# First stage of a two-layer backbone: order of the modulation loads, a last tile in two banks, rotary sines on another engine, a tie at the norm

## The chip, the cores and the metric

The kernel runs on one core of one Trainium2 chip. Its metric is device time in microseconds (us), the median of repeated executions. The engines are TensorE (PE in the profile), VectorE (DVE), ScalarE (ACT), GpSimd (POOL) and SyncE (SP), which here only issues loads and stores.

## The reference

A trunk of two layers on 1024 tokens of width 1024, with 256 context tokens. Layer 0 is windowed grouped-query attention with rotary positions and the context as a prefix; layer 1 is a Conformer convolution module. Each layer is an RMSNorm, shifted, scaled and gated by a linear map of the condition c (the "modulation"); a last RMSNorm ends it. Cut to what the change touches:

```python
shift, scale, gate = jnp.split((silu_c @ ada_w[i] + ada_b[i])[:, None, :], 3, axis=-1)
h_lat = modulate(rmsnorm(x, norm_g[i]), shift, scale)      # h * (1 + scale) + shift
proj = h_lat @ w_in                                         # layer 0
q = apply_rope(split_heads(proj[..., :q_end], N_Q_HEADS), cos, sin)
k = apply_rope(split_heads(proj[..., q_end:k_end], N_KV_HEADS), cos, sin)
v = split_heads(proj[..., k_end:v_end], N_KV_HEADS)
...
u = jax.nn.silu(layernorm(u, ln_g, ln_b))                   # layer 1
return (u * jax.nn.silu(z)) @ w_out
x = x + gate * y
```

## The kernel before, in words

**Numbers and tiles.** An fp32 product is made of three matmuls of split operands: high by high, low by high, high by low (`hh`, `hl` for activations, `whi`, `wlo` for weights). ScalarE writes a high part by a copy to the short form, VectorE or GpSimd the low part by a subtraction (`split_lo`, line 159). The width of 1024 is cut into eight tiles of 128 (`kt` 0 to 7), the tokens into two halves of 512.

**Program order.** Every instruction goes through one small wrapper, `InOrder`, so all of them carry its line, L89, in the profile; they are told apart by the names of their tiles. Where the wrapper is on, an engine's instructions keep the order in which the code is written: TensorE, VectorE and ScalarE through the whole first stage (`pin("PVA")`), TensorE alone after it (`pin("P")`), where a scheduler sets the order of the others. Each engine then works through its own queue strictly from the front.

**The loads of the first stage** (lines 318 to 345) stand in one queue on SP, 512 KB each: x rows 0 to 511 (four), `ada_load(0)` (the modulation's weights of tile 0, two transfers into `araw` pages), the first weight of the input projection (`wsA.load()`, a `wraw` page), `ada_load(1)`, the second and the third weight, `ada_load(2)` to `(5)`, x rows 512 to 1023, `ada_load(6)`, `(7)`, the context rows, and smaller things. Eight transfers are under way at a time: a further one is issued when the one eight places ahead has landed.

**The first half of the tokens** (lines 500 to 615). For each tile kt: `ada_row` multiplies the condition by the tile's modulation weights (16 small matmuls, `pso<-araw,c`, and a VectorE copy to an `arow` row); `turn` puts the x rows across by four transposes into one bank (`psg`); `ada_cols` turns the modulation row to columns (two pairs of tiny matmuls, `pso<-ident,arow`, and two VectorE rows that write `mod`); `x_tile` makes the modulated tile: ScalarE the high part `hh`, then VectorE the full value `hf` from the same bank, then VectorE `hl = hf - hh`; and `x_mm` adds its three products into the accumulators of the three weight chunks: 0 (k), 1 (q of the first group) and 2 (v). In between, `scale_rows` scales the x rows by their norm on ScalarE, `wsA.split` splits a weight (`whi` on ScalarE, `wlo` on VectorE, and from the fifth weight on `wlo` on GpSimd), and ScalarE squares the other rows for their norm.

**The second half** (lines 1172 to 1210) takes its x already turned (`xt`): VectorE `hf` (`x_f`), ScalarE `hh` (`x_h`), VectorE `hl` (`x_l`). Between its tiles stand two further streams. The context tiles (`c_tile`): two transposes, ScalarE `hf` and `hch`, VectorE `hcl`. And `rope` for the first half's k and q (lines 899 to 933): ScalarE copies the accumulator, SP swaps its halves by transfers (`rope_half`), VectorE multiplies by the cosine, GpSimd by the sine, and later, popped one at a time from the queue `ropes0` in tiles 4 to 7, VectorE adds the two, ScalarE writes the high part (`kh`, `qh`) and VectorE the low one (`kl`, `ql`). Then the first scores follow.

**The attention** (from line 1240) goes through heads and blocks: scores, softmax on the other engines, transposes, products with the values, and `fill(n)`, which puts n matmuls of the next projections (`psg`) into the gaps. At every fourth head (three times, at 267, 456 and 645 us) a *regroup* makes the next group's keys and values: `job("k")`, `job("v")`, `pv`, then `scores(*nxt)` and `vlate.pop(g)()`, which turns the last values by four transposes (`pso<-ident,vf_half`) and splits them (`vh`, `vl`).

**The norm of layer 1** (`layer_norm`, line 1467, for each half of the tokens): the squares are summed by VectorE, and across the partitions by PE (`pso<-ones,qa_half`); then VectorE `ms`, ScalarE the root `sq`, VectorE `rr` (reciprocal), `rq`, `rq`, `r`, and PE spreads r by `pso<-ident,r`. Around it runs the output projection, whose operands are split by `g_split` (line 1650; `gs` pages, high on ScalarE, low on VectorE) and `w_split` (`woh`, ScalarE).

## Time and profile before

| | |
|---|---|
| median of 3 runs | 1690.53 us (1690.23 to 1690.90) |
| the profiled execution, its own time | 1691.56 us |
| its span in the trace | 1689.8 us |
| granted TensorE clock | 0.999 |
| busy: PE, VectorE, ScalarE, GpSimd | 99%, 66%, 52%, 52% |
| transfers in the first fortieth of the span (42 us) | 385 GB/s, mean of the whole 145 |

A line of the trace reads: start in us from the start of the span, duration in us, engine, line, operation, what is written <- what is read, shape, how often, and in brackets how long the engine stood idle just before and what ended that idle time. SPq is SP's queue of issues. A line of waits reads: engine and tile, what was waited for, us in total, times, longest. A line of the chain of waits reads: start, duration, what was under way.

### The profile page before, as it was taken

The page shows a single profiled execution, that of the slowest core. Times are in us where ns is not written, and L with a number is a line of the kernel's source. Part 1 is how long each engine was busy: PE and PEld are TensorE (multiplying, and loading weights), DVE is VectorE, ACT ScalarE, POOL GpSimd, SP SyncE. Part 2 cuts the span into 40 slices and gives each one's busy share as a digit, 9 for nine tenths or more (in the row PEclk, how much of TensorE's full clock was granted, in tenths as well). Part 3 has the DMA queues.
Part 4 walks back from the last instruction along what each step waited for, and adds up shares of the span by engine and source line. Part 5 has one row for each costly group of instructions (what it writes and reads, how often), then busy time and mean ns, then how long its engine had stood idle before and what let it go on. Part 6 is the DMA issues. An engine that isn't in the chain of part 4 may idle for free.

```text
span 1689.8 us, 23975 instructions
## 1 busy us (share of the span) xinstructions
PE 1676.0 (99%) x8436; PEld 1413.9 (84%) x8436; DVE 1120.5 (66%) x2126; ACT 881.6 (52%) x1556; POOL 874.3 (52%) x724
## 2 busy tenths in 40 slices
PE   9999999999999999999999999999999999999998
PEld 6788888888888888888888888888888888888886
DVE  4756554656355654566324299999999999858832
ACT  5655543555355543556334365555665654566741
POOL 0166653666366663652101268999898887130400
PEclk9999999999999999999999999999999999999999
DMA  9424442544345443447976622020211212477881
GB/s 385 147 83 142 144 127 83 164 144 135 96 133 161 143 137 97 138 122 249 319 240 225 219 90 92 13 74 15 75 50 51 81 34 79 131 263 245 316 296 50
DMA packets 114776, 244.55 MB, mean 145 GB/s; under 512 B 11626, under 2 KB 36514, under 8 KB 114656
## 3 DMA queue, kind: packets, MB, share of 16 engines
q1 hardware_dynamic: 108576, 233.06, 41.0%
q10 hardware_dynamic: 6080, 9.97, 2.4%
q8 instruction: 66, 1.08, 0.3%
q14 instruction: 54, 0.44, 0.1%
HBM read 190.80 MB, written 41.69 MB: 138 GB/s over the span
## 4 chain that ended last, share of the span: by engine, by line
PE 92%; DMA 4%; DVE 2%; ACT 1%; issue 1%; SPq 0%; DVEq 0%; ACTq 0%
PE psg L89 50%; PE pss L89 21%; PE pso L89 21%; DMA wo_page<-in_conv_w_out_dram 1%; DMA araw_page<-in_k_ada_dram 1%; DMA x_page<-in_ctx_dram 1%; DMA x_page<-in_x_dram 1%; DVE pso L89 1%; DVE v_page L89 1%; DMA zsd<-sig_page 0%; DVE hf_page L89 0%; DMA wsum_raw<-in_ada_w_dram 0%; SPq L89 0%; ACT hh_page L89 0%; ACT gs_page L89 0%
## 5 line engine op out<-in xcount | busy, mean ns | idle before, releaser
L89 POOL TENSOR_TENSOR odd_half<-odd_half,prod_half 128x513 f32<-128x513 f32 (+2 forms) x252 | 315.0, 1258 | 22.0 <-ACT prod_half L89 8.5
L89 PE MATMUL psg<-hh_page,whi_page 128*128 128x512 f32 x600 | 235.5, 392 | 0.0
L89 PE MATMUL psg<-hl_page,whi_page 128*128 128x512 f32 x600 | 234.4, 391 | 0.0
L89 PE MATMUL psg<-hh_page,wlo_page 128*128 128x512 f32 x600 | 234.0, 390 | 0.0
L89 POOL TENSOR_TENSOR wlo_page<-wraw_page,whi_page 128x512 fp32r<-128x512 f32 (+1 forms) x104 | 172.1, 1670 | 113.7 <-ACT whi_page L89 52.9
L89 ACT ACTIVATE prod_half<-ubuf,dww 128x513 f32<-128x513 f32 (+2 forms) x252 | 165.7, 675 | 115.9 <-POOL odd_half L89 111.9
L89 PE MATMUL psg<-h2h_page,whi_page 128*128 128x512 f32 x464 | 181.9, 392 | 0.0
L89 PE MATMUL psg<-h2h_page,wlo_page 128*128 128x512 f32 x464 | 180.6, 389 | 0.0
L89 PE MATMUL psg<-h2l_page,whi_page 128*128 128x512 f32 x464 | 180.6, 389 | 0.0
L89 POOL TENSOR_SCALAR p_page<-p_page,sc 128x640 f32<-128x640 f32 (+1 forms) x128 | 100.2, 783 | 147.2 <-DVE sc L89 133.2
L89 DVE SCALAR_TENSOR_TENSOR pss<-ubuf,dww,pss 128x512 f32<-128x512 f32 (+3 forms) x270 | 172.4, 671 | 0.1
L89 DVE SCALAR_TENSOR_TENSOR pss<-ubuf,wsum,pss 128x512 f32<-128x512 f32 (+3 forms) x270 | 171.7, 671 | 0.2
L89 ACT ACTIVATE p_page<-p_page,sc 128x641 f32<-128x641 f32 (+1 forms) x128 | 102.9, 804 | 95.2 <-DVE sc L89 92.3
L89 ACT ACTIVATE pthi<-pss 128x512 fp32r<-128x512 f32 (+2 forms) x144 | 87.4, 619 | 111.0 <-PE pss L89 104.5
L89 DVE TENSOR_TENSOR ptlo<-pss,pthi 128x512 fp32r<-128x512 f32 (+2 forms) x144 | 101.8, 716 | 63.4 <-ACT pthi L89 62.2
L89 PEld LDWEIGHTS psg<-hh_page,wlo_page 128*128 128x128 f32 x600 | 112.6, 188 | 24.5
L89 PEld LDWEIGHTS psg<-hh_page,whi_page 128*128 128x128 f32 x600 | 112.8, 188 | 19.4
L89 PEld LDWEIGHTS psg<-hl_page,whi_page 128*128 128x128 f32 x600 | 112.8, 188 | 18.4
L89 POOL TENSOR_TENSOR rope_half<-rope_half,sin_page 128x512 f32<-128x512 f32 x40 | 52.1, 1302 | 142.1 <-DMA rope_half<-rope_half 68.8
L89 ACT ACTIVATE whi_page<-wraw_page 128x1024 fp32r<-128x1024 f32 x88 | 92.6, 1052 | 49.4 <-PE psg L89 21.6
L89 PE MATMUL pso<-h2h_page,whi_page 128*128 128x512 f32 x304 | 118.3, 389 | 0.0
L89 PE MATMUL pso<-h2l_page,whi_page 128*128 128x512 f32 x304 | 118.3, 389 | 0.0
(258 smaller groups left out, 4070.2 us busy)
## 6 DMA issues: line engine op xcount, KB each, us to landing
wraw_page<-in_k_wconv_dram SPq DMA_DIRECT2D x48, 512.0 KB, 3.2
wraw_page<-in_k_win_dram SPq DMA_DIRECT2D x40, 512.0 KB, 3.8
wo_page<-in_attn_w_out_dram SPq DMA_DIRECT2D x32, 512.0 KB, 6.2
wol_page<-wolA SPq DMA_DIRECT2D x32, 512.0 KB, 8.6
wo_page<-in_conv_w_out_dram SPq DMA_DIRECT2D x32, 512.0 KB, 7.3
wol_page<-wolC SPq DMA_DIRECT2D x32, 512.0 KB, 6.7
rope_half<-rope_half ACTq DMA_DIRECT2D x76, 128.0 KB, 2.4
araw_page<-in_k_ada_dram SPq DMA_DIRECT2D x16, 512.0 KB, 10.0
```

Source lines behind the costliest of these rows:

```text
L89: r = f(*a, **k)
```

## The change

It has seven parts. (1) `ada_load(2)` stands ahead of the third weight's load, and `ada_load(6)` between two pairs of x rows. (2) In the first half, the scaling of the last two x rows, tile 2's `ada_row` and its `ada_cols` stand ahead of the third weight's split, and tile 1's `ada_cols` stands one matmul earlier. (3) Tile 7's four transposes go into two banks, two each; ScalarE makes the high part of one half of the tokens while VectorE makes the full value of the other, then they swap, and one subtraction follows. (4) For the first half's k and q, the product with the sine is made by VectorE, in the popped pieces, which now are (product and sum) and (high and low part), and they are popped behind the context tiles. (5) The gate's first weight (z) is loaded and split one tile earlier. (6) At a regroup, the last values are turned and split only behind the next but one scores and three fills. (7) The low parts of `g_split` are tied to stand behind the layer norm's `ms`.

The places that matter, as the engines' queues have them. SP's queue in the first stage (araw: the modulation, two transfers per tile; wraw: the weights; x: token rows), before:

```order
L89 DMA wraw_page_109<-in_k_win_dram 128x1024
L89 DMA wraw_page_111<-in_k_win_dram 128x1024
L89 DMA araw_page_114<-in_k_ada_dram 128x1024
L89 DMA araw_page_115<-in_k_ada_dram 128x1024
L89 DMA araw_page_118<-in_k_ada_dram 128x1024
L89 DMA araw_page_119<-in_k_ada_dram 128x1024
```

and now:

```order
L89 DMA wraw_page_109<-in_k_win_dram 128x1024
L89 DMA araw_page_112<-in_k_ada_dram 128x1024
L89 DMA araw_page_113<-in_k_ada_dram 128x1024
L89 DMA wraw_page_116<-in_k_win_dram 128x1024
L89 DMA araw_page_118<-in_k_ada_dram 128x1024
L89 DMA araw_page_119<-in_k_ada_dram 128x1024
```

Tile 2's two transfers moved up by one place and the third weight down by two; tile 3's (118, 119) stay. VectorE's queue at tile 2, before:

```order
L89 COPY arow_half_113<-pso_321 128x256
L89 TENSOR_TENSOR wlo_page_317<-wraw_page_111,whi_page_316 128x1024
L89 TENSOR_SCALAR mod_177<-pso_338,bcol 128x2
L89 TENSOR_SCALAR mod_177<-pso_338,bcol,vt 128x2
L89 TENSOR_SCALAR hf_page_345<-psg_306,mod_177 128x512
L89 TENSOR_TENSOR hl_page_344<-hf_page_345,hh_page_343 128x512
```

and now:

```order
L89 COPY arow_half_111<-pso_318 128x256
L89 TENSOR_SCALAR mod_177<-pso_330,bcol 128x2
L89 TENSOR_SCALAR mod_177<-pso_330,bcol,vt 128x2
L89 TENSOR_TENSOR wlo_page_336<-wraw_page_116,whi_page_335 128x1024
L89 TENSOR_SCALAR hf_page_345<-psg_306,mod_177 128x512
L89 TENSOR_TENSOR hl_page_344<-hf_page_345,hh_page_343 128x512
```

The two `mod` rows moved ahead of the third weight's low part. VectorE's queue at the second norm (ms, rr, rq, r are the norm's; gs the output projection's splits), before:

```order
L89 TENSOR_TENSOR gs_page_14764<-v_page_13480,gs_page_14764 128x512
L89 TENSOR_SCALAR ms_789_14482<-pso_14477 128x4
L89 TENSOR_TENSOR gs_page_14659<-v_page_12324,gs_page_14659 128x512
L89 RECIPROCAL rr_791_14486<-sq_790_14484 128x4
L89 SCALAR_TENSOR_TENSOR rq_792_14488<-rr_791_14486 128x4
L89 TENSOR_TENSOR rq_792_14488<-rq_792_14488,ms_789_14482 128x4
L89 SCALAR_TENSOR_TENSOR r_793_14491<-rq_792_14488,rr_791_14486 128x4
L89 TENSOR_TENSOR gs_page_14695<-v_page_12784,gs_page_14695 128x512
```

and now (a page's number is higher by 3):

```order
L89 TENSOR_SCALAR ms_790_14485<-pso_14480 128x4
L89 TENSOR_TENSOR gs_page_14659<-v_page_12087,gs_page_14659 128x512
L89 TENSOR_TENSOR gs_page_14695<-v_page_12560,gs_page_14695 128x512
L89 TENSOR_TENSOR gs_page_14662<-v_page_12327,gs_page_14662 128x512
L89 TENSOR_TENSOR gs_page_14731<-v_page_13033,gs_page_14731 128x512
L89 TENSOR_TENSOR gs_page_14767<-v_page_13483,gs_page_14767 128x512
L89 RECIPROCAL rr_792_14489<-sq_791_14487 128x4
L89 SCALAR_TENSOR_TENSOR rq_793_14491<-rr_792_14489 128x4
```

Four splits that stood ahead of `ms` now stand behind it, so five stand between it and the reciprocal in place of one; on ScalarE the order there is unchanged.

```diff
--- before.py
+++ after.py
@@ -179,11 +179,13 @@
     def rstd_of(ssum, n, width, part=None):
         return rstd_end(rstd_root(ssum, n, width, part), width)
 
+    ms_at, anchor_ms = [], []
+
     def rstd_root(ssum, n, width, part=None):
 
         ms = small([P, width], name=f"ms{width}")
         if part is None:
-            V.tensor_scalar(out=ms, in0=ssum, scalar1=1.0 / n, scalar2=EPS, op0=ALU.mult, op1=ALU.add)
+            ms_at[:] = [V.tensor_scalar(out=ms, in0=ssum, scalar1=1.0 / n, scalar2=EPS, op0=ALU.mult, op1=ALU.add)]
         else:
             stt(ms, ssum, 1.0 / n, part, ALU.mult, ALU.add)
         sq = small([P, width], name=f"sq{width}")
@@ -320,8 +322,9 @@
     wsA.load()
     ada_load(1)
     wsA.load()
+    ada_load(2)
     wsA.load()
-    for kt in range(2, 6):
+    for kt in range(3, 6):
         ada_load(kt)
 
     cs = ctile([P, 40], F32, "cs")[:, 0:16]
@@ -333,8 +336,9 @@
     V.tensor_copy(bcol[:, 0:8], tp[:, 32:40])
     V.tensor_scalar(out=bcol[:, 8:16], in0=tp[:, 40:48], scalar1=1.0, scalar2=None, op0=ALU.add)
     hp.free(crow_pg)
-    xs1 = load_rows(x[0, 512:1024], 4)
+    xs1 = load_rows(x[0, 512:768], 2)
     ada_load(6)
+    xs1 += load_rows(x[0, 768:1024], 2)
     ada_load(7)
     cx = load_rows(ctx[0], 2)
     vec_pg = pg.alloc(F32, [P], "vecs")
@@ -428,6 +432,25 @@
         for i in range(len(ts)):
             PE.transpose(tp[:, i * P:(i + 1) * P], ts[i][:, kt * P:(kt + 1) * P], ident)
         return tp
+
+    def turn_apart(ts, kt, o):
+        for i in range(2):
+            PE.transpose(o[:, i * P:i * P + P], ts[i][:, kt * P:(kt + 1) * P], ident)
+        return o
+
+    def x_tile_apart(tps, kt):
+
+        Hh.append(pg.alloc(F32R, [1024], "hh"))
+        Hl.append(pg.alloc(F32R, [1024], "hl"))
+        f, m = pg.alloc(F32, [1024], "hf"), mods[kt]
+        h0, h1 = slice(0, 256), slice(256, 512)
+        with tc.high_priority():
+            for a, v, c, d in ((0, 1, h0, h1), (1, 0, h1, h0)):
+                act(Hh[kt][:, c], tps[a][:, 0:256], AF.Identity, scale=m[:, 1, 0:1], bias=m[:, 0, 0:1])
+                V.tensor_scalar(out=f[:, d], in0=tps[v][:, 0:256], scalar1=m[:, 1, 0:1], scalar2=m[:, 0, 0:1],
+                                op0=ALU.mult, op1=ALU.add)
+            split_lo(V, Hl[kt][:, 0:512], f[:, 0:512], Hh[kt][:, 0:512])
+        pg.free(f)
 
     def turn_scaled(kt, done=0, between=None):
         tp = ps_g()
@@ -517,8 +540,9 @@
     x_mm(0, 0, acc0, (0,), (0,))
     scale_rows(xs0[0:2], r0[:, 0:2], (A, A))
     ada_row(1)
-    x_mm(0, 0, acc0, (0,), (1, 2))
+    x_mm(0, 0, acc0, (0,), (1,))
     ada_cols(1)
+    x_mm(0, 0, acc0, (0,), (2,))
     wsA.split()
     x_tile(tp1, 1, 0, V)
     tp2 = turn_scaled(2, 2)
@@ -528,14 +552,13 @@
     x_mm(0, 0, acc0, (1,), (2,))
     x_mm(1, 0, acc0, (1,), (0,))
 
-    def second():
-        scale_rows(xs0[2:4], r0[:, 2:4], (A, A))
-        ada_row(2)
-
-    wsA.split(second)
-    x_mm(1, 0, acc0, (0, 1), (1, 2))
+    scale_rows(xs0[2:4], r0[:, 2:4], (A, A))
+    ada_row(2)
+    x_mm(1, 0, acc0, (0,), (1, 2))
+    ada_cols(2)
+    wsA.split()
+    x_mm(1, 0, acc0, (1,), (1, 2))
     x_mm(0, 0, acc0, (2,), (0, 1))
-    ada_cols(2)
     x_tile(tp2, 2, 0, V)
     pg.free(zer_r)
     ada_row(3)
@@ -549,18 +572,23 @@
         nx = kt + 1
         if 2 < kt < KT - 1:
             ada_row(nx)
-            tp = turn(xs0, nx, ps_g)
+            tp = turn(xs0, nx, ps_g) if nx < KT - 1 else turn_apart(xs0[0:2], nx, ps_g())
         if kt == 5:
             root1 = rstd_root(ss1, D, 4)
         if kt == KT - 1:
             x_mm(kt - 1, 0, acc0, (2,))
             turn_vecs()
         x_mm(kt, 0, acc0, (0,))
+        if nx == KT - 1:
+            tp = tp, turn_apart(xs0[2:4], nx, ps_o(0))
         if nx < KT:
             ada_cols(nx)
             if kt == 5:
                 r1 = rstd_end(root1, 4)
-            x_tile(tp, nx, 0, V)
+            if nx < KT - 1:
+                x_tile(tp, nx, 0, V)
+            else:
+                x_tile_apart(tp, nx)
         else:
             x_h(0)
             x_f(1)
@@ -905,7 +933,16 @@
         queue.dma_start(out=w[0:64], in_=e[64:128])
         queue.dma_start(out=w[64:128], in_=e[0:64])
         first = tt(V, r, o, cos[:, sl], ALU.mult)
-        tt(G, w, w, sin[:, sl], ALU.mult)
+        if ropes is None:
+            tt(G, w, w, sin[:, sl], ALU.mult)
+
+        def sine():
+            tt(V, w, w, sin[:, sl], ALU.mult)
+            tt(V, r, r, w, ALU.add)
+
+        def high_low():
+            act(d[0][:, sl], r, AF.Copy)
+            low()
 
         def add(behind=None):
             i = tt(eng if ropes is None and hold is None else V, r, r, w, ALU.add)
@@ -930,7 +967,7 @@
             add()
             low()
         else:
-            ropes.extend((add, low))
+            ropes.extend((sine, high_low))
 
     vlate = {}
 
@@ -1187,20 +1224,21 @@
             pg.free(rb_pg)
         if kt < 2:
             finished0(0, acc0, (kt,), ropes0)
-        if kt > 3 and ropes0:
-            ropes0.popleft()()
         if 0 < kt < 5:
             for _ in range(2):
                 b = (KT - len(ctodo)) % 3
                 c_tile(ctodo.popleft(), lambda: ps_o(b) if b < 2 else ps_g())
+        if kt > 3 and ropes0:
+            ropes0.popleft()()
         if kt == 5:
             for i in (1, 2):
                 d0[i].extend(target("kqv"[i], 0))
-            wsA.load()
+            wsA.split()
         if kt >= 6 and tails:
             tails.pop(0)()
+        if kt == 4:
+            wsA.load()
         if kt == 6:
-            wsA.split()
             ctx0("k", 0)
         if kt == 7:
             ctx0("v", 2, lambda: ps_o(1))
@@ -1246,7 +1284,12 @@
         if nxt and not regroup:
             scores(*nxt)
         if not regroup:
-            fill(15 if h and h % 4 == 0 and qb < 4 else FILL)
+            n = 15 if h and h % 4 == 0 and qb < 4 else FILL
+            if h // 4 in vlate and h:
+                fill(3)
+                n -= 3
+                vlate.pop(h // 4)()
+            fill(n)
         if pvq:
             pv(*pvq.popleft())
         if regroup:
@@ -1258,7 +1301,6 @@
             pv(h, 1)
             pg.free(*old[:3])
             scores(*nxt)
-            vlate.pop(g)()
             continue
         transposes(h, qb)
         if lstate[0] == "open" or h and (h % 4 < 3 or qb < LOWS):
@@ -1495,6 +1537,7 @@
         hp.free(qa)
         with tc.high_priority():
             r = rstd_of(o[:, 0:4], 1, 4)
+        anchor_ms[:] = ms_at
         yield "spread"
         rb = ps_o(bank)
         for b in range(4):
@@ -1652,7 +1695,7 @@
         if (h, k) not in gst:
             t = pg.alloc(F32R, [2, 2, 256], "gs")
             act(t[:, 0], vh(k, h), AF.Copy)
-            split_lo(V, t[:, 1], vh(k, h), t[:, 0])
+            after(split_lo(V, t[:, 1], vh(k, h), t[:, 0]), anchor_ms)
             gst[(h, k)] = t
             vdone(k, h)
```

## The prediction

> **What bounds the kernel now.** First the page: its shares of busy time.
>
> ```profile
> span 1689.8 us, 23975 instructions
> PE 1676.0 (99%) x8436; PEld 1413.9 (84%) x8436; DVE 1120.5 (66%) x2126; ACT 881.6 (52%) x1556; POOL 874.3 (52%) x724
> ```
>
> TensorE (PE) is idle for only 1689.8 − 1676.0 = 13.8 us. The change leaves the number and the shapes of its matmuls as they are, so it can only move the gaps between them. The second view is what PE waits for:
>
> ```profile
> PE pss L89 <- DVE hl_page L89: 1.2, 3, 0.6
> PE pso L89 <- ACT hf_page L89: 0.9, 2, 0.6
> PE pso L89 <- DVE r L89: 0.6, 1, 0.6
> PE pso L89 <- DVE oz_half L89: 0.5, 3, 0.2
> PE pso L89 <- DMA araw_page<-in_k_ada_dram: 0.5, 1, 0.5
> ```
>
> These lines sum to 3.7 us. They understate it: a matmul's row reaches past the start of the next. So third I read the timeline at each gap and count from start to start, less the step that is usual for the shape: 0.23 us between products of 128x512, 0.33 behind a group of small ones, 0.11 between transposes. The terms are in us of the profiled execution, 1691.56 us by its own time (span 1689.8, 1.76 around it). The runs shown have a median of 1690.53; since the gaps are what moves, the sum comes off either.
>
> **A. Tile 2's modulation ahead of the third weight (13 to 28 us).** PE first; then, from the chain of waits, the load that it waits for; then two of SP's issues, each of which waits for the landing eight places ahead in the queue.
>
> ```profile
> 22.24 0.64 PE L89 MATMUL pso<-araw_page,c_page 128*32 128x256 f32 x8 [0.45 <-DMA araw_page<-in_k_ada_dram]
> ...
> 27.69 0.50 PE L89 MATMUL pss<-hl_page,whi_page 128*128 128x512 f32 x1 [0.59 <-DVE hl_page L89]
> ```
>
> ```profile
> 10.69 11.51 DMA araw_page<-in_k_ada_dram
> ```
>
> ```profile
> 19.47 0.33 SPq L89 DMA_DIRECT2D x_page<-in_x_dram  x1
> ```
>
> ```profile
> 24.67 0.33 SPq L89 DMA_DIRECT2D x_page<-in_x_dram  x1
> ```
>
> Tile 2's second half landed at 10.69 + 11.51 = 22.20, its first at 19.47, tile 3's second at 24.67, two places behind 22.20: 1.24 a place. One place up, tile 2 is complete at 19.47 and PE doesn't stop at 22.24; the first eight of that group begin at 21.15 and sixteen take 1.0, so the next product comes at 22.15 for 22.81: 0.66 ahead. The third weight takes the place of 22.20. Now ScalarE, then VectorE:
>
> ```profile
> 20.09 1.05 ACT L89 ACTIVATE whi_page<-wraw_page 128x1024 fp32r<-128x1024 f32 x1
> 21.04 2.17 ACT L89 ACTIVATE x_page<-x_page,r 128x1024 f32<-128x1024 f32 x2
> 25.28 0.78 ACT L89 ACTIVATE hh_page<-psg,mod 128x512 fp32r<-128x512 f32 x1 [2.07 <-DVE mod L89]
> ```
>
> ```profile
> 26.09 0.81 DVE L89 TENSOR_SCALAR hf_page<-psg,mod 128x512 f32<-128x512 f32 x1 [0.85 <-ACT hh_page L89]
> 26.94 0.69 DVE L89 TENSOR_TENSOR hl_page<-hf_page,hh_page 128x512 fp32r<-128x512 f32 x1
> ```
>
> The scalings go first, 20.1 to 22.25; the weight has landed by then, its high part is done at 23.3, before PE reads it at 23.6. Tile 2's columns pass PE at 22.7 in place of 24.30, and hh starts 0.98 behind them as before: 23.7 to 24.5. VectorE splits the weight (1.2) from 23.7 to 24.9; hf and hl follow to 26.4 in place of 27.63. PE meanwhile wants tile 3's second half at 24.5 and gets it at 24.67, a new wait of 0.2; sixteen products, four transposes and three products later it asks for hl at 26.4, and the wait at 27.69 (0.99 start to start, 0.23 usual) is gone. The gain at this point is 27.69 − 26.45 = **1.2**. What comes late next? Tile 6's modulation, moved between the rows, lands eight places behind 24.67, near 34.6, and is asked for 1.2 earlier than before, near 37.0; in its old place, two further on, it would have come at 37.05, so this move is needed. The last two rows land at 35.8 and 37.05, ahead of their squares (36.8 and 37.8, by the same shift). Bounds: 0.4 if the irregular place (19.47 to 22.20 is 2.7 in place of 1.24) falls on tile 3 and PE stands there instead; 1.6 if tile 3's half comes a little early.
>
> **B. Tile 7 in two banks.**
>
> ```profile
> 47.36 0.81 DVE L89 TENSOR_SCALAR hf_page<-psg,mod 128x512 f32<-128x512 f32 x1 [0.93 <-ACT hh_page L89]
> 48.21 0.69 DVE L89 TENSOR_TENSOR hl_page<-hf_page,hh_page 128x512 fp32r<-128x512 f32 x1
> ```
>
> ```profile
> 48.95 0.50 PE L89 MATMUL pss<-hl_page,whi_page 128*128 128x512 f32 x1 [0.42 <-DVE hl_page L89]
> ```
>
> VectorE reads the bank only behind ScalarE (0.78 like the row at 25.28). With a bank each, both start at 46.5, take some 0.5 for half the width, and swap; hl starts near 47.65 for 48.21. PE's gap of 0.90 shrinks to its usual 0.33: **0.5 gained**, the fourth instruction hidden beside the other engine's; 0.2 if the halves queue.
>
> **C. Sine products on VectorE (57 to 72 us).** POOL, VectorE, ScalarE and PE in turn:
>
> ```profile
> 60.60 1.56 POOL L89 TENSOR_TENSOR rope_half<-rope_half,sin_page 128x512 f32<-128x512 f32 x1 [0.89 <-DMA rope_half<-rope_half]
> ```
>
> ```profile
> 59.03 1.29 DVE L89 TENSOR_TENSOR hcl_page<-hf_page,hch_page 128x256 fp32r<-128x256 f32 x2
> 60.25 0.74 DVE L89 SCALAR_TENSOR_TENSOR hl_page<-hf_page,mod,hh_page 128x512 fp32r<-128x512 f32 x1
> 60.91 1.79 DVE L89 SCALAR_TENSOR_TENSOR hf_page<-xt_page,mod,rb_page 128x512 f32<-128x512 f32 x1
> ```
>
> ```profile
> 68.02 0.63 ACT L89 ACTIVATE kh_page<-rope_page 128x512 fp32r<-128x512 f32 x1 [2.08 <-DVE rope_page L89]
> ```
>
> ```profile
> 62.99 0.38 PE L89 MATMUL pso<-ident,x_page 128*128 128x128 f32 x2
> 63.97 0.44 PE L89 MATMUL pso<-ident,x_page 128*128 128x128 f32 x2 [0.59 <-ACT hf_page L89]
> ...
> 69.16 0.66 PE L89 MATMUL pso<-ident,vf_half 128*128 128x128 f32 x4 [0.27 <-ACT hf_page L89]
> ```
>
> Beside POOL's sine, VectorE's 60.91 takes 1.79 where its like took 0.74, over 1 us lost; ScalarE's tile parts come late behind it, and PE stands at 63.97 (0.98 less two transposes, 0.76). The second gap, at 69.16 (0.66, 0.23 usual: 0.43), comes from kh, which waits 2.08 for a VectorE sum with the context's hf behind it; kh now stands behind all context tiles. A small gap between (0.25, near 66.5) goes with them. VectorE gets two products of 0.68 (a row of that shape is in E), but is given back 1 to 1.6 us of stretch, and the products stand behind what PE reads next. **1.4 gained**; 0.7 if only the first gap goes.
>
> The Trainium skill, "SBUF — State Buffer", section "SBUF: two separate sides", says that a GpSimd instruction and a VectorE one with two SBUF inputs shut each other out for the whole instruction. The stretched rows agree (1.79 against 0.74). By that rule the shutting out could come back at GpSimd's next task, a weight split; rival 2 prices that from rows.
>
> **D. The late values behind the next scores.** One of three places (the waits show 3):
>
> ```profile
> 267.21 0.28 PE L89 MATMUL pss<-kvc_page,ql_page 128*128 128x256 f32 x1
> 267.66 0.63 PE L89 MATMUL pso<-ident,vf_half 128*128 128x128 f32 x4 [0.16 <-DVE oz_half L89]
> ```
>
> 0.45 from start to start, 0.12 usual: 0.33. Six score products and three fills, 1.4 us, now cover the wait for the bank. Of 3 x 0.33 I take **0.9**; 0.3 if the scores find their own bank late twice. The values' own parts come 1.4 later; their first reader stands behind two further groups of products, so that costs nothing.
>
> **E. The tie at the norm.** ScalarE, then VectorE:
>
> ```profile
> 1557.78 1.15 ACT L89 ACTIVATE gs_page<-v_page 128x512 fp32r<-128x512 f32 x2
> ```
>
> ```profile
> 1559.05 0.15 DVE L89 TENSOR_SCALAR ms<-pso 128x4 f32<-128x4 f32 x1
> 1559.12 0.68 DVE L89 TENSOR_TENSOR gs_page<-v_page,gs_page 128x512 fp32r<-128x512 f32 x1
> 1560.01 0.18 DVE L89 RECIPROCAL rr<-sq 128x4 f32<-128x4 f32 x1 [0.20 <-ACT sq L89]
> ```
>
> ms goes ahead of five splits; the reciprocal stands behind all five, and ScalarE's root keeps its place in ScalarE's queue. The third split needs the second high part of the row at 1557.78, done at 1558.9, or 0.6 sooner if the queues before it gain what leaves VectorE. Three splits at 0.6 then end at 1560.1 to 1560.75, and r comes 0.1 to 0.75 later than now. PE has nothing ahead of its wait for r. **0.4 lost**; from 0.75 lost to 0.4 gained (all high parts early).
>
> **Sum:** 1.2 + 0.5 + 1.4 + 0.9 − 0.4 = 3.6. That gives 1690.53 − 3.6 = **1686.9 us** (profiled 1688.0, span 1686.2). PE releases all later work, so I see nothing that eats the gain.
>
> **Rivals.**
> 1. The loads only trade places: PE's wait at 22.24 moves to tile 3 or to the third weight, and A keeps its lower bound 0.4: 1687.7. For: all these loads share one full queue, and an irregular place exists. Against: from 24.67 on each load has room.
> 2. GpSimd's weight split holds VectorE's low part of q. PE reads it here, and a pair of such splits takes 2.53:
>
> ```profile
> 77.94 0.28 PE L89 MATMUL pss<-kh_page,ql_page 128*128 128x256 f32 x1
> ```
>
> ```profile
> 80.77 2.53 POOL L89 TENSOR_TENSOR wlo_page<-wraw_page,whi_page 128x512 fp32r<-128x512 f32 x2
> ```
>
> On this scale, less C, PE wants it at 76.5 and I have it ready near 75.1. A whole pair in the way leaves 2.53 − 1.4 = 1.1 lost: 1688.0. For: the stretched rows above. Against: it must start at the worst moment.
> 3. Slower. q's high part now stands in ScalarE's queue behind two weights, one of which is loaded late. From its landing, split, sine, sum and q's parts take some 5.2 us (1.05 + 1.2 + 2 x 0.68 + 0.6 + 0.68, and steps), and 76.5 is the time wanted: it decides at a landing of 71.3. Its page comes free near 63.6; issued then and as slow as the 11.51 above it lands at 75.1: 3.8 lost, and with E at its worst 1690.53 − 3.25 + 3.8 = 1691.1, slower. Against it: the page's median for such loads is 3.8 us:
>
> ```profile
> wraw_page<-in_k_win_dram SPq DMA_DIRECT2D x40, 512.0 KB, 3.8
> ```
>
> 4. The change doesn't do what it says where it ties the norm: r comes 0.75 later, and D gives only its 0.3: 1690.53 − 2.65 = 1687.9.
>
> **How the numbers follow.** My case 0.54; rival 1 0.14, rival 2 0.12, rival 3 0.10, rival 4 0.10. The worst terms sum to 0.4 + 0.2 + 0.7 + 0.3 − 0.75 = 0.85, the best to 1.6 + 0.6 + 1.5 + 1.0 + 0.4 = 5.1: the range is 1685.4 to 1689.7, and leaves out rival 3 and a remnant. A measurement of this kernel tells about 0.2%, 3.4 us, from no change: faster is below 1687.15, slower above 1693.9. My case lies 0.25 inside the first with its spread on both sides, so I give 0.54 to faster (part of my case, E or A better than taken), 0.40 to no change, 0.06 to slower (the bad end of rival 3 or one like it).
>
> **What would show it.** Right: no DMA wait of PE at 22, a short one at 24.5, none on hl near 26; no VectorE row stretched between 55 and 66; no oz_half line among PE's waits; r's line 0.9 or so. Wrong: PE waiting on a weight or on ql before 80 us, or a new gap in the scores of a regrouping.

## The result, and the profile after

The changed kernel takes **1686.97 us** (median; 1686.03 to 1688.57) beside 1690.95 (1690.12 to 1691.88) for the kernel before: a ratio of 0.9978, with an interval of 0.9970 to 0.9986. That is 3.98 us less (2.4 to 5.1); the forecast was 1686.9. A later measurement of the same two kernels gave 1687.53 beside 1691.36, again 0.9978 (0.9969 to 0.9987).

The profiled execution took 1686.54 us, 5.0 less than the one of before. Its page and what TensorE (PE) waits for:

```profile
span 1684.7 us, 23962 instructions
...
PE 1674.3 (99%) x8436; PEld 1413.2 (84%) x8436; DVE 1115.7 (66%) x2129; ACT 881.7 (52%) x1557; POOL 870.0 (52%) x722
```

```profile
PE pss L89 <- DVE zerr_page L89: 2.0, 1, 2.0
PE pss L89 <- DVE hl_page L89: 0.4, 2, 0.2
PE psg L89 <- DVE zs_page L89: 0.2, 1, 0.2
```

The lines on araw, on the context's hf, on oz_half, on r and on hh are gone; hl has lost one of its three. New is zs, at 780. The rest of this text asks which of these losses belong to the change, and which to the one execution that was traced.

For that I use one measure throughout. Every matmul of a trace is set beside the matmul at the same place in the program of the changed kernel's first trace, and its start is compared; the **lateness** is the median of these differences in a stretch. Where lateness rises from one stretch to the next, PE has lost time there. Columns are the place in the program, in us of the changed kernel's trace:

| kernel | 13 | 27 | 44 | 47 | 54 | 68 | 100 | 660 | 790 | 975 | 1557 |
|---|---|---|---|---|---|---|---|---|---|---|---|
| before | 0.88 | 1.84 | 1.80 | 2.00 | 1.98 | 3.52 | 3.51 | 4.42 | 4.20 | 4.20 | 5.04 |
| before, again (e8) | 0.66 | 1.87 | 1.83 | 2.04 | 2.01 | 3.55 | 3.55 | 4.46 | 4.21 | 5.61 | 5.61 |
| before with the tie (e5) | 0.61 | 1.41 | 1.36 | 1.57 | 1.56 | 3.08 | 3.07 | 4.06 | 3.82 | 5.25 | 5.25 |
| changed, again (e10) | 1.25 | 0.91 | 0.91 | 0.93 | 0.92 | 0.91 | 0.91 | 0.90 | 1.08 | 1.08 | 1.08 |
| without the tie (e1) | 0.81 | 0.58 | 0.57 | 0.59 | 0.57 | 0.57 | 0.54 | 0.53 | 0.75 | 2.15 | 2.15 |
| sine on GpSimd (e2) | 0.67 | 0.42 | 0.42 | 0.44 | 0.42 | 1.47 | 1.47 | 1.52 | 1.07 | 2.44 | 2.44 |
| old loads (e3) | 0.87 | 1.01 | 0.99 | 0.77 | 0.75 | 0.73 | 0.73 | 0.72 | 1.97 | 1.97 | 2.14 |
| one bank (e4) | 1.08 | 0.73 | 0.73 | 0.93 | 0.90 | 0.89 | 0.87 | 0.91 | 0.45 | 1.87 | 1.87 |
| old order of work (e6) | 1.33 | 1.66 | 1.64 | 1.65 | 1.62 | 1.62 | 1.60 | 1.60 | 1.88 | 3.22 | 3.22 |
| old regrouping (e7) | 0.81 | 0.47 | 0.45 | 0.47 | 0.44 | 0.44 | 0.43 | 1.34 | 1.17 | 2.64 | 2.64 |
| sum in PSUM (e9) | 0.62 | 0.40 | 0.40 | 0.41 | 0.41 | 0.41 | 0.41 | 0.41 | 0.58 | 0.58 | 0.58 |
| sum in PSUM, no tie (e11) | 0.68 | 0.78 | 0.77 | 0.78 | 0.80 | 0.78 | 0.75 | 0.75 | 0.30 | 0.30 | 0.30 |

Read a row for its steps, not for its level. The steps into the columns 13, 975 and, with one small exception (e3), 1557 turn out to differ between executions of one kernel. So does the step into 790 between kernels that don't differ there. The other steps follow the edits, but the step into 27 also carries the landing time of a load and scatters by 0.4.

### The profile page after: what moved, and what is told of

It reads as the page before. It is cut to its first block, busy times and chain, and to the rows that moved or that the text cites. A ratio compares the mean times of both kernels' runs of the same rounds, so it can differ in the third digit from the quotient of the medians.

```text
span 1684.7 us, 23962 instructions
## 1 busy us (share of the span) xinstructions
PE 1674.3 (99%) x8436; PEld 1413.2 (84%) x8436; DVE 1115.7 (66%) x2129; ACT 881.7 (52%) x1557; POOL 870.0 (52%) x722
## 3 DMA queue, kind: packets, MB, share of 16 engines
q8 instruction: 66, 1.08, 0.2%
## 4 chain that ended last, share of the span: by engine, by line
PE 97%; DMA 2%; ACT 0%; DVE 0%; SPq 0%; issue 0%; ACTq 0%
PE psg L89 51%; PE pss L89 25%; PE pso L89 22%; DMA araw_page<-in_k_ada_dram 1%; DMA wraw_page<-in_k_win_dram 0%; DMA wo_page<-in_attn_w_out_dram 0%; SPq L89 0%; ACT hh_page L89 0%; ACT p_page L89 0%; DVE x_page L89 0%; ACT x_page L89 0%; DVE oz_half L89 0%; DVE zs_page L89 0%; DVE hf_page L89 0%; ACT vf_half L89 0%
## 5 line engine op out<-in xcount | busy, mean ns | idle before, releaser
L89 PE MATMUL pso<-h2h_page,wlo_page 128*128 128x512 f32 x304 | 118.3, 389 | 0.0
```

Of the source, the lines that this page charges most:

```text
L89: r = f(*a, **k)
```

## The experiments

The theory was the sum of the prediction, each term in its own place: A in 13 to 28, B at 47, C in 57 to 72, D at three places from 264, E at the norm. Rivals were that A comes from the loads alone or from the engine order alone, that B, C or E are worth something else, and that the 5.0 of the two traces holds things that the change has nothing to do with.

### e3 and e6: the two halves of A

e3 puts the loads back in their old order and keeps the new order of work:

```diff
-    ada_load(2)
     wsA.load()
-    for kt in range(3, 6):
+    for kt in range(2, 6):
...
-    xs1 = load_rows(x[0, 512:768], 2)
+    xs1 = load_rows(x[0, 512:1024], 4)
     ada_load(6)
-    xs1 += load_rows(x[0, 768:1024], 2)
```

> The changed kernel with the loads in the old order (third weight ahead of tile 2, tile 6 behind all rows), instructions on the engines as changed. Theory: the loads' order makes the gain; tile 2's second half lands near 22.0 where PE asks at 20.7, a wait of 1.3, of which some 0.4 is got back since the waits behind it go: PE 0.7 to 1.0 later at tile 3's columns. Rival: the order on the engines makes the gain; then 0.3 or less.

e6 keeps the new loads and puts the order of work back:

```diff
-    x_mm(0, 0, acc0, (0,), (1,))
+    x_mm(0, 0, acc0, (0,), (1, 2))
     ada_cols(1)
-    x_mm(0, 0, acc0, (0,), (2,))
...
-    scale_rows(xs0[2:4], r0[:, 2:4], (A, A))
-    ada_row(2)
-    x_mm(1, 0, acc0, (0,), (1, 2))
+    def second():
+        scale_rows(xs0[2:4], r0[:, 2:4], (A, A))
+        ada_row(2)
+
+    wsA.split(second)
+    x_mm(1, 0, acc0, (0, 1), (1, 2))
+    x_mm(0, 0, acc0, (2,), (0, 1))
     ada_cols(2)
-    wsA.split()
-    x_mm(1, 0, acc0, (1,), (1, 2))
-    x_mm(0, 0, acc0, (2,), (0, 1))
```

> The changed kernel with the loads in the new order, but the instructions of tiles 1 and 2 on the engines as before (third weight's split ahead of the row scaling and ahead of tile 2's mod rows). Theory: the weight now lands behind tile 2's modulation, so ScalarE stands for it until 21.7, scales until 24.9, and only then makes tile 2's high part; the low part comes near 27.3 where PE asks at 26: PE 0.8 to 1.2 later at tile 3's columns, so the loads need the order of the engines with them. Rival: the loads' order alone carries the gain; then 0.3 or less.

First the changed kernel on PE. The columns are the start, the time and the form; a bracket gives the idle time in front of a row and what ended it.

```profile
20.19 1.07 PE L89 MATMUL pso<-araw_page,c_page 128*32 128x256 f32 x16
...
23.48 1.33 PE L89 MATMUL pso<-araw_page,c_page 128*32 128x256 f32 x16
...
25.93 0.40 PE L89 MATMUL pss<-hl_page,whi_page 128*128 128x512 f32 x1
```

Tile 2's sixteen products run through (20.19). Tile 3's take 1.33 for 1.07, the short wait that was forecast (0.26 for 0.2), and hl is there when PE asks at 25.93. Now PE in e3, then in e6:

```profile
21.98 0.64 PE L89 MATMUL pso<-araw_page,c_page 128*32 128x256 f32 x8 [0.27 <-DMA araw_page<-in_k_ada_dram]
```

```profile
27.50 0.50 PE L89 MATMUL pss<-hl_page,whi_page 128*128 128x512 f32 x1 [0.59 <-DVE hl_page L89]
```

With the old loads the wait on the modulation is back (0.91 from 21.07 to 21.98, where eight products take 0.46) and hl is in time. With the old order of work the loads are in time and hl is late by as much as before. The order of work also removes a wait that the prediction doesn't name, one on tile 1's high part. In before, and then in e6:

```profile
20.25 0.51 PE L89 MATMUL pss<-hh_page,whi_page 128*128 128x512 f32 x1 [0.20 <-ACT hh_page L89]
```

```profile
20.69 0.50 PE L89 MATMUL pss<-hh_page,whi_page 128*128 128x512 f32 x1 [0.20 <-ACT hh_page L89]
```

It is there in all four traces with the old order of work (before, e5, e6, e8), 0.60 from start to start for 0.32, and in none with the new one.

The sizes are less certain than the waits. From column 13 to 27, the eight traces with the whole of A change by -0.35 to +0.10, by -0.20 in the mean. The +0.10 is e11: tile 3's products take 1.35 from 24.25 on there, and 1.07 from 24.30 on in e1, so in e11 that load landed later. Against this mean, e3 (+0.14) loses 0.3 and e6 (+0.33) loses 0.5; against the traces with the most similar start, 0.4 (e1, e7) and 0.7 (e10). Both lie below what was expected of them, 0.7 to 1.0 and 0.8 to 1.2, and the 0.3 of e3 alone is within the scatter. For the whole of A, the three traces of before rise by 0.96, 1.21 and 0.80, by 0.99 in the mean: 0.99 + 0.20 = **1.2**. So each half removes waits of its own, neither makes the whole gain, and neither rival holds.

### e4: B undone

```diff
-            tp = turn(xs0, nx, ps_g) if nx < KT - 1 else turn_apart(xs0[0:2], nx, ps_g())
+            tp = turn(xs0, nx, ps_g)
...
-            if nx < KT - 1:
-                x_tile(tp, nx, 0, V)
-            else:
-                x_tile_apart(tp, nx)
+            x_tile(tp, nx, 0, V)
```

> The changed kernel with tile 7 in one bank as before. Theory: two banks were worth only what the two traces show, 0.67 of excess ahead of tile 7's low product against 0.50, so PE comes 0.1 to 0.25 later. Rival, the prediction's term: 0.5 later.

Lateness rises by 0.20 at 47 (0.73 to 0.93), as in all three traces of before. B is worth **0.2**, the lower bound, not 0.5. Tile 7 in the changed kernel, on all engines:

```profile
44.68 0.54 DVE L89 TENSOR_SCALAR hf_page<-pso,mod 128x256 f32<-128x256 f32 x1
44.76 0.56 ACT L89 ACTIVATE hh_page<-psg,mod 128x256 fp32r<-128x256 f32 x1 [0.48 <-DVE mod L89]
...
45.36 0.55 DVE L89 TENSOR_SCALAR hf_page<-psg,mod 128x256 f32<-128x256 f32 x1
...
45.63 0.56 ACT L89 ACTIVATE hh_page<-pso,mod 128x256 fp32r<-128x256 f32 x1 [0.30 <-issue]
...
46.23 0.69 DVE L89 TENSOR_TENSOR hl_page<-hf_page,hh_page 128x512 fp32r<-128x512 f32 x1 [0.32 <-ACT hh_page L89]
...
46.98 0.50 PE L89 MATMUL pss<-hl_page,whi_page 128*128 128x512 f32 x1 [0.23 <-DVE hl_page L89]
```

And in e4, the two reads of the one bank, by ScalarE and by VectorE:

```profile
45.48 0.78 ACT L89 ACTIVATE hh_page<-psg,mod 128x512 fp32r<-128x512 f32 x1 [0.48 <-DVE mod L89]
...
46.30 0.81 DVE L89 TENSOR_SCALAR hf_page<-psg,mod 128x512 f32<-128x512 f32 x1 [0.93 <-ACT hh_page L89]
```

Half the width takes 0.54 to 0.56, not half of 0.78 or 0.81, so two halves cost 1.1 (the prediction had 0.5 each); and ScalarE's second half starts 0.30 after its first ended, with nothing that the profile shows to wait for. hl starts 1.47 behind ScalarE's first read here, and 1.66 behind it in e4 (47.14). In e3 the 0.30 did not occur, hl starts 1.23 behind ScalarE's first read, and PE's gap there fell from 0.50 to 0.28, by itself: so 0.4 is what B could give, and the idle 0.30 is most of what is missing. Why it is there in the eight other traces with two banks stays open.

### e2: C undone

```diff
-        if ropes is None:
-            tt(G, w, w, sin[:, sl], ALU.mult)
+        tt(G, w, w, sin[:, sl], ALU.mult)
...
         def sine():
-            tt(V, w, w, sin[:, sl], ALU.mult)
             tt(V, r, r, w, ALU.add)
```

> The changed kernel with the two sine products back on GpSimd, ahead of the popped pieces; the pops stay behind the context tiles. Theory: GpSimd's 1.3 to 1.6 us rows stretch VectorE's again (1.8 for 0.75) and PE's gap near 62 to 64 (0.76) and the small one behind it (0.25) return; the gap at the last values (0.43) stays gone, since kh still comes behind the context. PE 0.8 to 1.0 later from there. Rival: the place of the pops made the gain; then under 0.2.

The sines are back on GpSimd, where they stood before; the popped pieces keep their new place, behind the context tiles. GpSimd, VectorE and PE in e2:

```profile
59.04 1.55 POOL L89 TENSOR_TENSOR rope_half<-rope_half,sin_page 128x512 f32<-128x512 f32 x1 [0.89 <-DMA rope_half<-rope_half]
```

```profile
59.35 1.78 DVE L89 SCALAR_TENSOR_TENSOR hf_page<-xt_page,mod,rb_page 128x512 f32<-128x512 f32 x1
```

```profile
62.40 0.44 PE L89 MATMUL pso<-ident,x_page 128*128 128x128 f32 x2 [0.58 <-ACT hf_page L89]
```

In the changed kernel VectorE's rows of that form, and its sine:

```profile
58.70 0.75 DVE L89 SCALAR_TENSOR_TENSOR hf_page<-xt_page,mod,rb_page 128x512 f32<-128x512 f32 x1
...
65.09 0.68 DVE L89 TENSOR_TENSOR rope_half<-rope_half,sin_page 128x512 f32<-128x512 f32 x1
```

GpSimd's sine stretches VectorE's row from 0.75 to 1.78, and PE stands 1.05 behind it (lateness 0.42 to 1.47): the gaps that begin at 61.5 and 64.7, of 0.74 and 0.24, that the prediction priced at 0.76 and 0.25. The third gap, 0.43, does not come back, and in e2 the context tiles still go ahead of kh. That it is this order which removed it was not tested by a run of its own. The whole of C, from column 54 to 68, is 1.54 in before, 1.54 in e8 and 1.52 in e5: **1.5** for 1.4 forecast. Part 5 of the change, the gate's first weight one tile earlier, has no run of its own either; between columns 68 and 100 no row moves by more than 0.03, so no cost or gain of it shows there.

### e7: D undone

```diff
-            n = 15 if h and h % 4 == 0 and qb < 4 else FILL
-            if h // 4 in vlate and h:
-                fill(3)
-                n -= 3
-                vlate.pop(h // 4)()
-            fill(n)
+            fill(15 if h and h % 4 == 0 and qb < 4 else FILL)
...
             scores(*nxt)
+            vlate.pop(g)()
             continue
```

> The changed kernel with the last values turned and split straight behind the regroup's scores, as before. Theory: three gaps of 0.33 return ahead of the value transposes, PE 0.9 to 1.0 later behind the third. Rival: the shift of the first stage already changed these places; then under 0.3.

PE in e7, then the same place in the changed kernel:

```profile
264.14 0.28 PE L89 MATMUL pss<-kvc_page,ql_page 128*128 128x256 f32 x1
264.58 0.63 PE L89 MATMUL pso<-ident,vf_half 128*128 128x128 f32 x4 [0.17 <-DVE oz_half L89]
```

```profile
263.71 0.28 PE L89 MATMUL pss<-kvc_page,ql_page 128*128 128x256 f32 x1
263.83 0.34 PE L89 MATMUL pss<-kh_page,qh_page 128*128 128x384 f32 x1
```

0.44 from start to start against 0.12. Lateness rises by 0.91 between 100 and 660, in three equal steps; **0.9** as forecast, and no score waits for its own bank.

### e1, e5 and e8: the tie, and before once more

e1 takes the tie out of the changed kernel, e5 puts it alone into the kernel before, and e8 is the kernel before as it was.

```diff
-            after(split_lo(V, t[:, 1], vh(k, h), t[:, 0]), anchor_ms)
+            split_lo(V, t[:, 1], vh(k, h), t[:, 0])
```

> The changed kernel without the tie of the low parts behind ms, all else kept. Theory: the tie takes four splits of 0.6 us off VectorE ahead of the squares' sum; that chain (sum, its copy, a table load, a weight row, the page it frees, the next weight's load, the root) then runs over 2 us earlier against PE. Without the tie PE waits for r again, 0.6 to 0.8 from start to start, and PE's end moves 0.8 later. Rival: the earlier chain is a late effect of the other parts; then no wait for r comes back and the end stays within 0.1.

> The kernel before with the tie alone. Theory after the first four runs: the tie is not what took PE's wait for r away (without it r still came 1.3 us ahead of PE's demand); r hangs on the landing of the output weights in ScalarE's queue, which differs from execution to execution by 2 us. The tie then shortens the squares' chain (first sum to its copy) by some 0.5 us, and lengthens ms to r from 1.56 to 4.2, and PE's wait for r lies anywhere from 0 to 0.8 as in the kernel before. Rival: the tie does it; then r comes about 1 us ahead of PE's demand with it in every execution and PE's end moves 0.8 earlier.

> The kernel before, unchanged, for a second trace. Theory: four of its gaps are of the execution and not of the kernel: the warm-up products' slow steps (0 to 1 us), the wait in the out projection near 784 (0 to 1.6), the stop near 967 (0 or 1.3, by whether GpSimd's weight split or VectorE's sum starts first), and the wait for r near 1560 (0 to 0.8); at least two of them differ by over 0.3 from the first trace, while the gaps of the first stage and of the regroups repeat within 0.1. Rival: all gaps repeat within 0.1.

The root and its reciprocal on their way to PE, in the changed kernel (ScalarE, VectorE, PE) and in e1:

```profile
1553.22 0.19 ACT L89 ACTIVATE sq<-ms 128x4 f32<-128x4 f32 x1
```

```profile
1554.80 0.16 DVE L89 SCALAR_TENSOR_TENSOR r<-rq,rr 128x4 f32<-128x4 f32 x1
```

```profile
1555.94 1.05 PE L89 MATMUL pso<-ident,r 128*128 128x128 f32 x8
```

```profile
1555.81 0.19 ACT L89 ACTIVATE sq<-ms 128x4 f32<-128x4 f32 x1
```

```profile
1556.64 0.16 DVE L89 SCALAR_TENSOR_TENSOR r<-rq,rr 128x4 f32<-128x4 f32 x1
```

```profile
1558.09 1.05 PE L89 MATMUL pso<-ident,r 128*128 128x128 f32 x8
```

From the root's start to r it is 1.74 with the tie and 0.99 without, so behind the root r comes 0.75 later, as the prediction's worse bound had it. But PE comes for r only 0.98 and 1.29 after it is done, so this costs nothing, and the wait of 0.6 to 0.8 that was expected of e1 doesn't come back. Lateness does not move from 975 to 1557 in e1, e5 or e8. PE at the same place in before and in e8, which are one kernel:

```profile
1560.92 1.13 PE L89 MATMUL pso<-ident,r 128*128 128x128 f32 x8 [0.61 <-DVE r L89]
```

```profile
1561.56 1.05 PE L89 MATMUL pso<-ident,r 128*128 128x128 f32 x8
```

In e8, r is 1.41 ahead of PE, while in the first trace of before PE waits for it; that wait (0.84 in the table) was one execution's. In the nine traces with the tie, r is 0.15 (e3) to 1.5 (e7) ahead without any edit near it; in three of the four without, 1.3 to 1.6. The 0.15 of e3 is as little as in before, where PE was waiting, and lateness rises by 0.17 there. So **E is 0** in these traces, 0.17 lost in e3, not 0.4 lost. Whether the tie also prevents a wait as long as that of before, four traces without it are too few to say.

e8 also shows that the first stage repeats less well than was expected: its wait on the modulation's load is 0.68, and 0.45 in the first trace of before. The regroups and B's and C's gaps do repeat within 0.1.

### e9, e10 and e11: the stop at 967

Seven of the first ten traces have a stop of 1.2 to 1.3 at one product between 790 and 975 (1.34 to 1.47 in lateness, with the slower steps behind it), on either side of the change. VectorE, GpSimd and PE in e1:

```profile
960.39 2.90 DVE L89 TENSOR_TENSOR x_page<-x_page,xr_page 128x512 f32<-128x512 f32 x1
```

```profile
960.33 7.70 POOL L89 TENSOR_TENSOR wlo_page<-wraw_page,whi_page 128x1024 fp32r<-128x1024 f32 x3 [28.98 <-DMA wraw_page<-in_k_wconv_dram]
```

```profile
968.89 0.50 PE L89 MATMUL pss<-woh_page,ozh_page 128*128 128x512 f32 x1 [1.11 <-DVE x_page L89]
```

VectorE and GpSimd at the same place in the changed kernel:

```profile
959.64 0.69 DVE L89 TENSOR_TENSOR x_page<-x_page,xr_page 128x512 f32<-128x512 f32 x1
```

```profile
959.76 7.66 POOL L89 TENSOR_TENSOR wlo_page<-wraw_page,whi_page 128x1024 fp32r<-128x1024 f32 x3 [29.16 <-DMA wraw_page<-in_k_wconv_dram]
```

VectorE adds the residual while GpSimd starts to split a weight. Where GpSimd is first, by 0.06 here, the addition takes 2.90; where VectorE is first, by 0.12, it takes 0.69, and GpSimd's first split 2.83 in place of 2.40 (its single rows in the two traces). In all eleven traces with this addition the order of the two starts decides (0.00 to 0.21 apart; at 0.00 it went either way). The Trainium skill, "SBUF — State Buffer", section "SBUF: two separate sides", says that of a GpSimd instruction and a VectorE one with two SBUF inputs the one that starts first holds the port for its whole length; the eleven traces agree.

e9 leaves the product in PSUM, so that the addition has one SBUF input only; e10 is the changed kernel again, e11 is e9 without the tie (e1's edit).

```diff
-        tt(V, t, acc, gbc0[0][:, ns], ALU.mult)
-        tt(G if b % 2 and s < len(subs) - 1 else V, t, t, xr[b // 2][:, b % 2], ALU.add)
+        u = acc if s == len(subs) - 1 and b == 0 else t
+        tt(V, u, acc, gbc0[0][:, ns], ALU.mult)
+        tt(G if b % 2 and s < len(subs) - 1 else V, t, u, xr[b // 2][:, b % 2], ALU.add)
```

> The changed kernel, with one sum of the output projection's last quarter (rows of block 0) read from PSUM: VectorE leaves the product with the gate in its PSUM bank and adds the residual tile to it from there, so that the addition has one operand in SBUF instead of two. Theory (the stop of 1.2 to 1.3 us at 967 is VectorE's addition of two SBUF operands held by GpSimd's run of weight splits, decided by which of the two starts first): the addition takes 0.69 us in every execution, also when GpSimd has begun, as the product of a PSUM and an SBUF operand did at 965.08 in the changed kernel (0.68 with GpSimd busy from 959.76 to 967.42); the stop is gone, TensorE's lateness does not rise between 940 and 975, and the median falls by the stop times its share of executions (7 of 10 traces: 0.9), to 1685.9 to 1686.4; beside the changed kernel of this call 0.5 to 1.2 less. Rival (the stop is VectorE's queue being long, or the bank's late release by it, whoever holds the port): the addition stays stretched to about 2.9 or TensorE still stops by 1.2, and the time is the changed kernel's, 1686.9 or so.

> The changed kernel as it is, a second time, as the ground for the two others of this call and for what differs from one execution to the next. Theory (warm-up, the stop at 967 and the load-paced stop at 779 differ by execution, the rest does not): the trace shows the first stage as before within the warm-up's 0 to 1.3, the stop at 967 with 7 chances in 10, and r ahead of TensorE or within 0.8 of it; median 1686.5 to 1687.4. Rival (the stop at 967 belongs to the variants, not to the changed kernel): no stop here, and the three kernels' medians agree within 0.3.

> The kernel with the sum in PSUM, without the tie at the norm. Theory (the tie moves the root and with it r by 0.6 to 0.8, and r is 0.8 to 1.5 ahead of TensorE in most executions, so that the tie is worth nothing either way): the same time as the kernel with the sum in PSUM and the tie, within 0.3; root to r about 1.0 instead of 1.6. Rival 1 (the tie costs what it delays r by): 0.4 to 0.8 faster. Rival 2 (the tie saves the late r of 0.78 that the first trace of the kernel before shows): 0.4 to 0.8 slower, and a wait of TensorE on r in the trace.

VectorE and GpSimd in e11:

```profile
959.95 0.69 DVE L89 TENSOR_TENSOR x_page<-pss,xr_page 128x512 f32<-128x512 f32 x1
```

```profile
959.83 7.25 POOL L89 TENSOR_TENSOR wlo_page<-wraw_page,whi_page 128x1024 fp32r<-128x1024 f32 x3 [28.92 <-DMA wraw_page<-in_k_wconv_dram]
```

Here GpSimd is first by 0.12, and the addition takes 0.69 all the same: the mechanism of the stop is shown, though by this one execution (in e9 VectorE was first, by 0.03). But the time does not follow. e9 takes 1687.84 us (1686.4 to 1688.32), e11 1687.11 (1686.7 to 1688.07), the changed kernel of e10 1687.53 (1686.8 to 1689.35), with ratios to before of 0.9978 (0.9968 to 0.9987), 0.9975 (0.9964 to 0.9986) and 0.9978. The 0.5 to 1.2 expected of e9 were not there, and e10's trace has no stop either, like the first of the changed kernel. How often the stop comes in executions that are not traced I can't say; it is worth less on the median than 7 of 10 times 1.25. In e9 and e11, r is 1.3 and 1.6 ahead of PE, with the tie and without; the 0.7 between their medians is more than the 0.3 expected, but lies inside their ranges, and whether the tie costs or saves anything in other executions stays open.

### What differs from one execution to the next

Column 13 is over before the first place where the change moves work; in e1 and e2 it also holds 0.3 to 0.4 of a wait on tile 0's load. The 28 zero products in front of the first stage, on PE in before, in the changed kernel and in e6:

```profile
4.25 8.25 PE L89 MATMUL pss<-zerr_page 128*128 128x512 f32 x28
```

```profile
4.26 7.36 PE L89 MATMUL pss<-zerr_page 128*128 128x512 f32 x28
```

```profile
4.26 8.69 PE L89 MATMUL pss<-zerr_page 128*128 128x512 f32 x28
```

Their step is 0.43 us at first and 0.23 later, and the change of pace comes between 5.7 and 8.7 us, after 6 to 13 slow steps, while the profile gives the granted clock as 1.00 throughout (read in before and in the changed kernel, from 2 to 12 us): 0 to 1.33 of lateness. An execution that is late from the start waits less for tile 3's load; e10 takes up 0.34 there. The Trainium skill, "TensorE: Matmul & The Clock Gate", section "Part 1: The HAM clock gate (the "warmup" mystery)", says that the number of slow matmuls at the start differs from run to run; these traces agree. Column 790 is a load of an output weight. ScalarE, then PE, in e3:

```profile
778.36 1.06 ACT L89 ACTIVATE woh_page<-wo_page 128x1024 fp32r<-128x1024 f32 x1 [3.69 <-DMA wo_page<-in_attn_w_out_dram]
```

```profile
781.76 0.50 PE L89 MATMUL psg<-woh_page,ozh_page 128*128 128x512 f32 x1 [1.41 <-DVE zs_page L89]
```

The load comes late, ScalarE's next copy queues behind its split, and zs behind that: 0 to 1.6 of PE's time. It shows in five of the ten traces of the changed kernel and its variants and in none of the three of before, so that the change makes it more frequent is not excluded.

The times of e1 to e4, one each, were 1688.68, 1688.98, 1688.68 and 1688.41 beside 1692.37 for before; of e5 to e8 1691.79, 1689.74, 1689.17 and 1692.15 beside 1692.31. They move by as much from execution to execution as a single edit is worth, so the readings above rest on the steps of lateness and on the rows.

## Why the prediction was right

The terms, forecast and measured, in us: **A** 1.2 and 1.2; **B** 0.5 and 0.2; **C** 1.4 and 1.5; **D** 0.9 and 0.9; **E** 0.4 lost and 0. The sums are 3.6 and 3.8, for 3.98 and 3.83 between the medians. That the forecast time is met within 0.1 is partly luck, twice over. B and E were wrong in opposite directions, by 0.3 and 0.4. And the kernel before came 0.42 slower in this measurement than the 1690.53 that the forecast starts from, while the saving was 0.38 larger than forecast.

- A: the waits moved as worked out from the queue's places: tile 2's load in time, a new short wait on tile 3's second half, hl in time. Both the loads and the order of the work were needed. The wait on tile 1's hh went too, which the prediction did not count. Tile 6's load and the last rows caused no wait; but "so this move is needed" is not borne out, since e3 leaves tile 6's load in its old place and has no wait on it either. Rival 1, with 0.4 left of A, is refuted: 1.2 came, and no DMA line is left among PE's waits.
- B: the step that failed is "take some 0.5 for half the width, and swap; hl starts near 47.65 for 48.21". A half takes 0.54 to 0.56, which is a little more, but ScalarE stands for 0.30 between its halves, and hl starts 1.47 behind the first read in place of 1.15. Why ScalarE stands is open.
- C: the stretched row and its two gaps came out at the prices given, and kh's gap is gone. Rival 2 did not come: PE waits for no ql before 80. Rival 3 did not come either: between 50 and 100 PE has no gap over 0.2 in either trace of the changed kernel, so q's high part delays nobody.
- D: three times 0.3, covered by the scores.
- E: that r comes 0.75 later behind the root, with all the splits ahead of it, was right. The step that failed is "PE has nothing ahead of its wait for r". It was read from one trace in which r was late; in the others r has room, 0.15 to 1.6. Rival 4 took its price from the same step.

The traced pair differs by more than the medians, 5.0 for 4.0. The 1.1 more are the warm-up (0.88, of which 0.34 was taken up) and the wait for r (0.84), less 0.22 at 779. The first two are noise of the execution, as e10 and e8 show; for the third this is likely, but not shown.

## What to carry to other kernels

Price a change by the gaps of the busiest engine, counted from start to start, and for each gap ask by another execution of the same kernel whether it is there every time; here that moved one term from 0.4 to nothing. Setting two traces side by side, instruction by instruction, and looking for the places where the lateness steps shows each term of a few tenths of a us, where the times scatter by 1 to 2.5 us. Halving an instruction to let two engines swap gains less than the halves' times promise: here a half cost 0.55 of 0.8, and 0.30 of idle time between the halves took more of the gain than that.

## What the runs showed of the hardware that was not expected

An addition that VectorE starts 0.06 us behind a weight split of GpSimd takes 2.90 us instead of 0.69, and stops PE for 1.2 to 1.3 us, while 0.12 ahead it costs PE nothing; with one of its operands in PSUM it takes 0.69 even when it starts 0.12 behind. The start of TensorE at full pace (0.23 us a step for 0.43) came between 5.7 and 8.7 us from one execution to the next, so that the first 13 us of this kernel carry up to 1.3 us that no edit explains.
